# Attention of a decoder step on one core: from single heads to pairs of heads, with the score products cut to 64 rows

## The chip, the cores and the metric

The kernel is one program on one core of a Trainium2 chip. The metric is the time of one execution on the device in microseconds (us), as a median of several runs. The engines work side by side, each through its own list of instructions in a fixed order, and wait for each other through semaphores: TensorE (PE in the profile; PEld is its loading of weights), VectorE (DVE), ScalarE (ACT), GpSimd (POOL) and SyncE (SP), which here issues most DMAs.

## The reference

One layer of a decoder for a prompt of 1024 tokens and 8 samples of 8 new tokens. After the input projection each of 8 heads of 64 channels attends over the prompt. Three dilated window branches are merged by their softmax denominators, which is the same as one softmax over all earlier keys with an added table (bias plus the logarithm of the number of branches that see the key):

```python
    q = rms_norm(q, q_g) * (HEAD_DIM ** -0.5)
    k = rms_norm(k, k_g)
...
        attn = _merge_branches([_dilated_prompt(q, k, v, w, d, rel_bias) for w, d in DILATED_BRANCHES])
...
    mix = jnp.concatenate([attn, pool], axis=-1).astype(x.dtype) @ w_out
    x = x + gate1 * mix
```

The samples attend over a cache of 2048 past rows each, and the rest is a pooling path, an output projection, and a block of two large products (1024 to 4096 channels and back).

## The kernel before, in words

Everything is stored with channels on the 128 partitions. `qT[hp]` and `kT[hp]` hold two heads each, head 2*hp on partitions 0 to 63 and the odd one on 64 to 127. Large products are made in a one-pass form of float32 (F32R) from a high and a low part of each operand; products of plain float32 take two passes over the array, transposes one.

The stage that matters here begins behind the input projection and ends with the first product of the output projection (`oa`, L243). It runs over 32 units, each one head `h` and one group `g` of 256 queries (blocks 2g and 2g+1 of 128):

- `head_prep` makes the parts of q and k for the next head. `qs` holds the high part of q on the head's 64 partitions and its low part on the other 64, `kh` the high part of k on both (the second copy comes by a DMA, L487), `kl` the low part of k and zeros. So qs with kh and qs with kl are two products over 128 rows.
- `unit_S` makes the scores of 128 queries against all keys up to them: L620 and L621 into a PSUM bank (tag `S`, six banks, shared with transposes and the samples' work). `logits` (L536, VectorE) adds the bias tile `fs` of the head and keeps the row maximum, `softmax_tail` (L530, ScalarE) takes the exponential and its row sum, L625 puts the reciprocal on a diagonal `dg`.
- `unit_V` transposes the exponentials (L636), copies them out of PSUM (L639, ScalarE) and multiplies with the values (L641): 64 output channels, so that the two query blocks of the unit stand in two halves of the array's columns (output partitions 0 to 63 and 64 to 127). L644 spreads the reciprocal sums in the same way, L646 copies them, L650 multiplies and writes the result over `qT`.
- One step of the samples' attention goes between: `sample_S` (products of 32 output rows, four column groups, L557) and `sample_V` (L582 transposes, L590 products in four column groups).

The loop issues S of a unit, then V of the unit before it. This is not yet the order on the engines: a scheduler reorders the instructions when the program is built, by its own estimate of when each is ready. `load_bias` (L506) loads 512 KB of the table into `fs`, two buffers, one head ahead. `wp`, the weights of the pooling path's last product (L670, twelve products that fill the end of the stage), is loaded at the start of the stage. `split_mix` makes the high and low parts that the output projection reads.

In what follows a tiling is named as the profile names it, rows x columns of the array that a product takes: 128*128 (S and transposes), 128*64 (V), 128*32 (samples).

## Time and profile before

| what | value |
|---|---|
| median of 3 runs | 1380.88 us (1378.78 to 1387.12) |
| profiled execution | 1385.69 us |
| its span, first to last instruction | 1383.9 us |
| instructions in the span | 22069 |
| TensorE busy | 1323.1 us, 96% |
| mean granted clock of TensorE | 0.981 of 2.4 GHz |

The span and the profiled execution's own time differ by what lies around the instructions. Busy time of TensorE is a union of modelled spans, and its tail after the last column counts as busy; so a busy TensorE can still be one that changes from one tiling to another. Some records of products are missing from a trace, and a row that stands for "x4" may be three of them.

### The profile page before, as it was taken

Reading aid. Unit: us, or ns where it says so; the run is one execution under the profiler, and the core shown is the slowest. Engines: PE = TensorE matmul, PEld = TensorE weight load, DVE = VectorE, ACT = ScalarE, POOL = GpSimd, SP = SyncE. Lnnn points to the kernel's source line nnn. Section 1 sums busy time; section 2 is a strip of 40 time slices with the busy share of each in tenths; the row PEclk is TensorE's granted clock in tenths of the full one; section 3 lists DMA queues with packets and bytes.
Section 4 is the critical chain, followed back from the end, with each engine's and each line's share of the span. In section 5 each row is a group of like instructions: output and inputs, shape, how many; then the busy total and the mean of one; then the engine's idle time right before and its main releaser. Section 6 shows DMA issues by size and latency. Waiting matters only on the chain.

```text
span 1383.9 us, 22069 instructions
## 1 busy us (share of the span) xinstructions
PE 1323.1 (96%) x9284; PEld 1133.3 (82%) x9284; DVE 609.9 (44%) x1266; ACT 404.1 (29%) x708; POOL 142.2 (10%) x200
## 2 busy tenths in 40 slices
PE   3799999798999999999999999999999999999998
PEld 1486868586777768999999999999999999999998
DVE  5644142116767775577332433433433324334333
ACT  5232121125677763435202202112012012021120
POOL 3102004322223200000000000000000000000000
PEclk9799999899999999999999999999999999999999
DMA  9684331949867825481961541721814515411002
GB/s 302 214 148 141 122 122 62 146 129 345 268 234 240 286 80 193 135 283 61 348 203 46 186 148 46 258 76 45 275 46 135 199 46 186 148 46 46 31 33 97
DMA packets 59074, 213.10 MB, mean 154 GB/s; under 512 B 15056, under 2 KB 17104, under 8 KB 57952
## 3 DMA queue, kind: packets, MB, share of 16 engines
q1 hardware_dynamic: 55088, 138.82, 32.3%
q0 software_dynamic: 3888, 72.87, 16.4%
q8 instruction: 73, 1.20, 0.4%
q14 instruction: 25, 0.20, 0.0%
HBM read 199.15 MB, written 77.27 MB: 200 GB/s over the span
## 4 chain that ended last, share of the span: by engine, by line
PE 89%; DMA 4%; ACT 2%; DVE 2%; issue 2%; SPq 1%; POOL 0%; ACTq 0%; DVEq 0%
PE dn L243 9%; PE dn L245 9%; PE dn L247 9%; PE up L247 9%; PE up L243 9%; PE up L245 9%; PE z L243 5%; PE z L247 4%; PE z L245 4%; PE po L641 2%; DMA wa<-in_w_ada 2%; PE pt L636 2%; PE sl L557 1%; PE pa L101 1%; PE ob L245 1%
## 5 line engine op out<-in xcount | busy, mean ns | idle before, releaser
L723 DVE SCALAR_TENSOR_TENSOR X<-dn,aT,X 128x512 f32<-128x512 f32 (+2 forms) x192 | 98.4, 567 | 204.6 <-PE dn L247 204.6
L755 POOL COPY mark<-fh 128x1 f32<-128x1 f32 x7 | 8.5, 1219 | 562.2 <-ACT fh L822 562.2
L823 DVE TENSOR_TENSOR fl<-r,fh 128x1088 fp32r<-128x1088 f32 x32 | 41.3, 1292 | 35.5 <-ACT fh L822 35.5
L530 ACT ACTIVATE L<-L,m 128x128 f32<-128x128 f32 (+3 forms) x64 | 49.8, 778 | 22.2 <-DVE m L536 22.0
L641 PE MATMUL po<-PT,vtok 128*64 128x128 f32 x576 | 52.2, 287 | 4.1 <-ACT PT L639 3.4
L641 PEld LDWEIGHTS po<-PT,vtok 128*64 128x64 f32 x576 | 33.7, 136 | 23.4 <-ACT PT L639 12.9
L822 ACT CAST fh<-r 128x1088 fp32r<-128x1088 f32 x32 | 35.4, 1106 | 44.0 <-DVE r L819 44.0
L101 PE MATMUL pa<-wa,cs 128*32 128x256 f32 x384 | 31.5, 414 | 15.0 <-DMA wa<-in_w_ada 14.9
L639 ACT COPY PT<-pt 128x512 f32<-128x512 f32 (+1 forms) x80 | 40.2, 541 | 16.6 <-PE pt L636 16.4
L245 PE MATMUL dn<-fh,wd_3l 128*128 128x288 f32 (+1 forms) x192 | 43.4, 328 | 0.0
L243 PE MATMUL dn<-fh,wd_3h 128*128 128x288 f32 (+1 forms) x192 | 43.4, 328 | 0.0
L247 PE MATMUL dn<-fl,wd_3h 128*128 128x288 f32 (+1 forms) x192 | 43.4, 328 | 0.0
L243 PE MATMUL dn<-fh,wd_1h 128*128 128x288 f32 (+1 forms) x192 | 42.5, 328 | 0.0
L245 PE MATMUL dn<-fh,wd_1l 128*128 128x288 f32 (+1 forms) x192 | 42.5, 328 | 0.0
L247 PE MATMUL dn<-fl,wd_1h 128*128 128x288 f32 (+1 forms) x192 | 42.3, 328 | 0.0
L245 PE MATMUL dn<-fh,wd_0l 128*128 128x288 f32 (+1 forms) x192 | 42.3, 328 | 0.0
L636 PE MATMUL pt<-cpk,L 128*128 128x128 f32 x288 | 41.6, 281 | 0.7 <-ACT L L530 0.4
L243 PE MATMUL dn<-fh,wd_0h 128*128 128x288 f32 (+1 forms) x192 | 42.2, 328 | 0.0
L243 PE MATMUL dn<-fh,wd_2h 128*128 128x288 f32 (+1 forms) x192 | 42.2, 328 | 0.0
L245 PE MATMUL dn<-fh,wd_2l 128*128 128x288 f32 (+1 forms) x192 | 42.2, 328 | 0.0
L247 PE MATMUL dn<-fl,wd_2h 128*128 128x288 f32 (+1 forms) x192 | 42.2, 328 | 0.0
L247 PE MATMUL dn<-fl,wd_0h 128*128 128x288 f32 (+1 forms) x192 | 42.1, 328 | 0.0
(953 smaller groups left out, 3505.9 us busy)
## 6 DMA issues: line engine op xcount, KB each, us to landing
out_kw<-in_cache_k POOLq DMA_DIRECT2D x8, 4080.0 KB, 16.1
out_vw<-in_cache_v POOLq DMA_DIRECT2D x8, 4080.0 KB, 29.0
wa<-in_w_ada SPq DMA_DIRECT2D x48, 512.0 KB, 5.7
kc<-in_kc SPq DMA_DIRECT2D x40, 512.0 KB, 5.8
vc<-in_vc SPq DMA_DIRECT2D x40, 512.0 KB, 5.7
x<-in_xT SPq DMA_DIRECT2D x8, 544.0 KB, 8.3
X<-in_xT SPq DMA_DIRECT2D x8, 544.0 KB, 7.9
fs<-gscr SPq DMA_DIRECT2D x8, 512.0 KB, 6.4
```

Source lines behind the costliest of these rows:

```text
L101: ins = mm(pa[32 * g:32 * g + 32, :256], cs[:, k, :], t[:, g // 2, (g % 2) * 256:(g % 2 + 1) * 256], start=(k == 0), stop=(k == KD - 1))
L243: mm(pt[:, :n], wh[:, kw], xh(k, c0, n), start=st, stop=False)
L245: mm(pt[:, :n], wl[:, kw], xh(k, c0, n), start=False, stop=False)
L247: mm(pt[:, :n], wh[:, kw], xl(k, c0, n), start=False, stop=sp)
L530: last["act"] = S.activation(L[:, :n], L[:, :n], AF.Exp, bias=negm, scale=-1.0, accum_out=sm)
L557: mm(pt[32 * hp:32 * hp + 32, c0:c0 + 256], qz[:, hp, b, :], kch[:, hp, :], start=True, stop=True)
L636: nc.tensor.transpose(pt[:, n * P:(n + 1) * P], Ls[ii][:, j * P:(j + 1) * P], ident)
L639: S.copy(PT[:, :w], pt[:, :w])
L641: mm(po[E * ii:E * ii + E, :P], v_blk(j, h * E, E), PT[:, n * P:(n + 1) * P], start=(j == 0), stop=(j == 2 * g + ii))
L723: V.scalar_tensor_tensor(X[:, m, c0:c0 + npr], pt[:, :npr], aT[:, base + m, 0:1], X[:, m, c0:c0 + npr], ALU.mult, ALU.add)
L822: S.copy(fh, r)
L823: V.tensor_sub(fl, r, f(fh))
```

## The change

The unit becomes a pair of heads `hp` and a group of 256 queries (16 units in place of 32).

- S: three products over 64 rows (high q with high k, high q with low k, low q with high k) in place of two over 128. Head 0 of the pair takes the upper half of the array's rows, head 1 the lower half, each into a bank of its own. The copy of `kh` by DMA and the zeros in `kl` go; the parts are made for both heads at once on 128 partitions.
- V: the halves of the columns now stand for the two heads, and a product takes both query blocks of the unit, 256 wide (128 for the last key block). `dg` is made in one instruction for two heads and two blocks, and reciprocal, copy and multiplication come once in a unit.
- The exponentials of a unit lie in one tile, with one buffer for even and one for odd `g`; `dg` and `bc` have one buffer. Both `fs` buffers belong to the pair in work, and the loads for the next pair are written in the pair's second unit.
- The samples' steps are dealt out anew (three or four in a unit), `wp` is loaded behind the attention, and the memory for descriptors of software DMAs is halved.

```diff
-    kls = [wpool.tile([P, SEQ], F32R, tag="wf", name=f"kl{a}", bufs=NWF) for a in range(2)]
-    for a in range(2):
-        V.memset(f(kls[a][E - a * E:2 * E - a * E, :]), 0.0)
-
-    def head_prep(h, pieces):
-
-        hp, r0 = h // 2, (h % 2) * E
-        a, b = slice(r0, r0 + E), slice(E - r0, 2 * E - r0)
-        q, k, kl = qT[hp], kT[hp], kls[h % 2]
-        qs, kh = (wpool.tile([P, SEQ], F32R, tag="wf", name=f"{n}{h}", bufs=NWF) for n in ("qs", "kh"))
-        stacks[h] = (qs, kh, kl)
+
+    def pair_prep(hp, pieces):
+
+        q, k = qT[hp], kT[hp]
+        kh, qh, ql = [wpool.tile([P, SEQ], F32R, tag="wf", name=f"{n}{hp}", bufs=NWF) for n in ("kh", "qh", "ql")]
+        kl = nat(f"kl{hp}", F32R)
+        stacks[hp] = kh, kl, qh, ql
         w = SEQ // pieces
         for c0 in range(0, SEQ, w):
             c = slice(c0, c0 + w)
-            S.copy(kh[a, c], k[a, c])
-            nc.sync.dma_start(f(kh[b, c]), f(kh[a, c]))
-            S.copy(qs[a, c], q[a, c])
-            G.tensor_sub(kl[a, c], k[a, c], f(kh[a, c]))
-            G.tensor_sub(qs[b, c], q[a, c], f(qs[a, c]))
+            S.copy(kh[:, c], k[:, c])
+            S.copy(qh[:, c], q[:, c])
+            G.tensor_sub(kl[:, c], k[:, c], f(kh[:, c]))
+            G.tensor_sub(ql[:, c], q[:, c], f(qh[:, c]))
             yield
 
-    for _ in head_prep(0, 2):
+    for _ in pair_prep(0, 2):
...
-        fs = att.tile([P, FW], F32, tag="fs", name=f"fs{h}", bufs=2)
+        fs = att.tile([P, FW], F32, tag="fs", name=f"fs{h}", bufs=NFS)
...
+    load_bias(1)
...
-    def unit_S(h, g):
-        qs, kh, kl = stacks[h]
-        fs = biases[h]
-        out = []
-        dg = att.tile([P, 2 * P], F32, tag="dg", name=f"dg{h}_{g}", bufs=2)
+    def unit_S(hp, g):
+
+        kh, kl, qh, ql = stacks[hp]
+        Ls = {}
+        LL = att.tile([P, 2, (4 * g + 3) * P], F32, tag=f"L{g % 2}", name=f"L{hp}_{g}", bufs=1)
+        sm = att.tile([P, 4], F32, tag="sm4", name=f"sm{hp}_{g}", bufs=4)
         for ii in range(2):
             qi = 2 * g + ii
             nk = (qi + 1) * P
-            L = att.tile([P, SEQ], F32, tag="L", name=f"L{h}_{qi}", bufs=NL)
-            m = None
             n = nk if nk <= 512 else nk // 2
+            nm = max(n, 256)
+            qc = slice(qi * P, (qi + 1) * P)
+            ms = [None, None]
+            for a in range(2):
+                Ls[a, ii] = LL[:, a, ii * (nk - P):ii * (nk - P) + nk]
             for c0 in range(0, nk, n):
-                pt = ps(f"S{h}_{qi}_{c0}", "S")
-                nm = max(n, 256)
-                mm(pt[:, :nm], qs[:, qi * P:(qi + 1) * P], kh[:, c0:c0 + nm], start=True, stop=False)
-                mm(pt[:, :nm], qs[:, qi * P:(qi + 1) * P], kl[:, c0:c0 + nm], start=False, stop=True)
+                pts = [ps(f"S{hp}_{a}_{qi}_{c0}", "S") for a in range(2)]
+                for x, (w, m) in enumerate(((qh, kh), (qh, kl), (ql, kh))):
+                    for a in range(2):
+                        r = slice(a * E, (a + 1) * E)
+                        mm(pts[a][:, :nm], w[r, qc], m[r, c0:c0 + nm], start=(x == 0), stop=(x == 2))
                 b0 = (7 - qi) * P + c0
-                m = logits(L, c0, n, pt[:, :n], fs[:, b0:b0 + n], m, f"m{h}_{qi}_{c0}")
-            rv = softmax_tail(L, nk, m, f"p{h}_{qi}")
-            V.tensor_scalar_mul(dg[:, ii * P:(ii + 1) * P], ident, rv)
-            out.append(L)
-        return out, dg
-
-    def unit_V(h, g, Ls, dg):
-        hp, r0 = h // 2, (h % 2) * E
-        po = ps(f"po{h}_{g}", "po")
+                for a in range(2):
+                    ms[a] = logits(Ls[a, ii], c0, n, pts[a][:, :n], biases[2 * hp + a][:, b0:b0 + n], ms[a],
+                                   f"m{hp}_{a}_{qi}_{c0}")
+            for a in range(2):
+                softmax_tail(Ls[a, ii], nk, ms[a], sm[:, 2 * a + ii:2 * a + ii + 1])
+        rv = att.tile([P, 4], F32, tag="sm4", name=f"rv{hp}_{g}", bufs=4)
+        V.reciprocal(rv, sm)
+        dg = att.tile([P, 4, P], F32, tag="dg", name=f"dg{hp}_{g}", bufs=1)
+        V.tensor_tensor(dg, ident.unsqueeze(1).to_broadcast([P, 4, P]), rv.unsqueeze(2).to_broadcast([P, 4, P]), ALU.mult)
+        return Ls, dg
+
+    def unit_V(hp, g, Ls, dg):
+        po = ps(f"po{hp}_{g}", "po")
         for jp in range(g + 1):
-            pt = ps(f"pt{h}_{g}_{jp}", "S")
-            blocks = [(2 * jp + jj, ii) for jj in range(2) for ii in range(2) if 2 * jp + jj <= 2 * g + ii]
-            for n, (j, ii) in enumerate(blocks):
-                nc.tensor.transpose(pt[:, n * P:(n + 1) * P], Ls[ii][:, j * P:(j + 1) * P], ident)
-            PT = att.tile([P, 512], F32, tag="PT", name=f"PT{h}_{g}_{jp}", bufs=NPT)
-            w = len(blocks) * P
-            S.copy(PT[:, :w], pt[:, :w])
-            for n, (j, ii) in enumerate(blocks):
-                mm(po[E * ii:E * ii + E, :P], v_blk(j, h * E, E), PT[:, n * P:(n + 1) * P],
-                   start=(j == 0), stop=(j == 2 * g + ii))
-        for ii in range(2):
-            mm(po[E * ii:E * ii + E, P:2 * P], ones[:, :E], dg[:, ii * P:(ii + 1) * P], start=True, stop=True)
-        bc = att.tile([P, P], F32, tag="bc", name=f"bc{h}_{g}", bufs=2)
-        S.copy(bc, po[:, P:2 * P])
+            PTs = []
+            js = [(2 * jp + jj, [ii for ii in range(2) if 2 * jp + jj <= 2 * g + ii]) for jj in range(2)]
+            for a in range(2):
+                pt = ps(f"pt{hp}_{a}_{g}_{jp}", "S")
+                n = 0
+                for j, iis in js:
+                    for ii in iis:
+                        nc.tensor.transpose(pt[:, n * P:(n + 1) * P], Ls[a, ii][:, j * P:(j + 1) * P], ident)
+                        n += 1
+                PT = att.tile([P, 512], F32, tag="PT", name=f"PT{hp}_{a}_{g}_{jp}", bufs=NPT)
+                S.copy(PT[:, :n * P], pt[:, :n * P])
+                PTs.append(PT)
+            n = 0
+            for j, iis in js:
+                w = len(iis) * P
+                for a in range(2):
+                    mm(po[E * a:E * a + E, iis[0] * P:2 * P], v_blk(j, (2 * hp + a) * E, E), PTs[a][:, n:n + w],
+                       start=(j == 0), stop=(j == 2 * g + 1))
+                n += w
+        for a in range(2):
+            mm(po[E * a:E * a + E, 2 * P:4 * P], ones[:, :E], dg[:, 2 * a:2 * a + 2, :].rearrange("p s c -> p (s c)"),
+               start=True, stop=True)
+        bc = att.tile([P, 2 * P], F32, tag="bc", name=f"bc{hp}_{g}", bufs=1)
+        S.copy(bc, po[:, 2 * P:])
         mix = qT[hp]
-        for ii in range(2):
-            c = slice((2 * g + ii) * P, (2 * g + ii + 1) * P)
-            V.tensor_tensor(mix[r0:r0 + E, c], po[E * ii:E * ii + E, :P], bc[E * ii:E * ii + E], ALU.mult)
-        if h % 2 and g % 2:
-            if g == 1:
-                mixh[hp], mixl[hp] = nat(f"mixh{hp}", F32R), nat(f"mixl{hp}", F32R)
-            c = slice((g - 1) * 2 * P, (g + 1) * 2 * P)
-            split_mix(hp, c, mix[:, c], G)
+        c = slice(g * 2 * P, (g + 1) * 2 * P)
+        V.tensor_tensor(mix[:, c], po[:, :2 * P], bc, ALU.mult)
+        if g == 3:
+            mixh[hp], mixl[hp] = nat(f"mixh{hp}", F32R), nat(f"mixl{hp}", F32R)
+            for c in (slice(0, 512), slice(512, 1024)):
+                split_mix(hp, c, mix[:, c], G)
 
...
-    wp = att.tile([P, 4, P], F32, tag="wp", name="wp")
-    nc.sync.dma_start(wp, i["wpT"])
...
-    units = [(h, g) for h in range(H) for g in range(4)]
+    units = [(hp, g) for hp in range(HP) for g in range(4)]
     ready = []
-    for n, (h, g) in enumerate(units):
+    s_, v_ = [sample_S(b) for b in range(NB)], [sample_V(b) for b in range(NB)]
+    steps = [s_[0]] * 3 + [s_[1]] * 3 + [v_[0]] * 3
+    for b in range(1, NB):
+        for _ in range(3):
+            steps += ([s_[b + 1]] if b + 1 < NB else []) + [v_[b]]
+    steps = iter(steps)
+
+    def sample_steps(n):
+        for it in itertools.islice(steps, n):
+            next(it, None)
+
+    for hp, g in units:
         if g == 0:
-            if h + 1 < H:
-                load_bias(h + 1)
-            prep = head_prep(h + 1, 4) if h + 1 < H else iter(())
-            sS = itertools.chain(*(sample_S(b) for b in ((0, 1) if h == 0 else (h + 1,)) if b < NB))
-            sV = sample_V(h)
-        ready.append((h, g, *unit_S(h, g)))
-        for _ in range(2 if h == 0 else 1):
-            next(sS, None)
+            prep = pair_prep(hp + 1, 4) if hp + 1 < HP else iter(())
+        if g == 1 and hp + 1 < HP:
+            load_bias(2 * hp + 2)
+            load_bias(2 * hp + 3)
+        ready.append((hp, g, *unit_S(hp, g)))
+        sample_steps((1, 2, 2, 2)[g])
         if len(ready) > 1:
             unit_V(*ready.pop(0))
-        if h or g:
-            next(sV, None)
+        sample_steps((1, 1, 1, 2)[g])
         with tc.issue_after(last["act"].ins):
             next(prep, None)
-    next(sV, None)
     unit_V(*ready.pop(0))
+    sample_steps(48)
     for hp in range(HP):
         sv = attnS[:, hp].rearrange("p b t -> p (b t)")
         split_mix(hp, slice(SEQ, T), sv, V)
+    wp = wpool.tile([P, 4, P], F32, tag="raw", name="wp", bufs=NRAW)
+    nc.sync.dma_start(wp, i["wpT"])
...
-NL = 4
+NFS = 2
...
+    nc = _bacc.Bacc("TRN2", target_bir_lowering=False, num_devices=1, dynamic_dma_scratch_size=8192)
```

TensorE, the scores of query blocks 6 and 7 of the first head (before) or pair (after), between V products of the group before (names: `S_6_0` is block 6, keys from 0, and behind the change `S_0_6_0` that of head 0 in the pair; `po` is V's result, `PT` the copied transposes, `PT_0_1_0` of head 0, group 1, first four blocks; `x4` stands for four products). Before:

```order
L620 MATMUL S_6_0_2652<-kh_2313,qs_2312 128x448
L621 MATMUL S_6_0_2652<-kl_2308,qs_2312 128x448
L641 MATMUL po_1_2591<-PT_1_0_2597,vtok_2041 64x128 x4
L620 MATMUL S_6_448_2657<-kh_2313,qs_2312 128x448
L621 MATMUL S_6_448_2657<-kl_2308,qs_2312 128x448
L620 MATMUL S_7_0_2668<-kh_2313,qs_2312 128x512
L621 MATMUL S_7_0_2668<-kl_2308,qs_2312 128x512
L641 MATMUL po_1_2591<-PT_1_1_2607,vtok_2041 64x128 x3
L644 MATMUL po_1_2591<-dg_1_2415,cpk 64x128 x2
L620 MATMUL S_7_512_2673<-kh_2313,qs_2312 128x512
L621 MATMUL S_7_512_2673<-kl_2308,qs_2312 128x512
```

After:

```order
L621 MATMUL S_0_6_0_2715<-kh_2308,qh_2309 128x448
L621 MATMUL S_0_6_0_2715<-kl_2311,qh_2309 128x448
L621 MATMUL S_0_6_0_2715<-kh_2308,ql_2310 128x448
L653 MATMUL po_1_2642<-PT_0_1_0_2648,vtok_2041 64x256
L621 MATMUL S_1_6_0_2716<-kh_2308,qh_2309 128x448
L621 MATMUL S_1_6_0_2716<-kl_2311,qh_2309 128x448
L621 MATMUL S_1_6_0_2716<-kh_2308,ql_2310 128x448
L653 MATMUL po_1_2642<-PT_1_1_0_2655,vtok_2041 64x256
L653 MATMUL po_1_2642<-PT_0_1_0_2648,vtok_2041 64x256
L653 MATMUL po_1_2642<-PT_1_1_0_2655,vtok_2041 64x256
L621 MATMUL S_0_6_448_2727<-kh_2308,qh_2309 128x448
```

Before, a row of V products holds both halves of the columns. After, three products of one head stand in a row, then those of the other, and V's first product for head 0 stands alone between them.

SyncE, where the bias tiles of the third and fourth head are loaded (`fs2`, `fs3`; the digit behind `kc` and `vc` is the sample). Before, where head 1 is in work:

```order
L579 DMA vc1_0_2843<-in_vc 128x1024
L579 DMA vc1_1_2845<-in_vc 128x1024
L579 DMA vc1_2_2931<-in_vc 128x1024
L506 DMA fs2_2752<-gscr_101 128x1x1024
L487 DMA kh1_2409<-kh1_2409 64x256
L554 DMA kc2_4_2997<-in_kc 128x1024
L554 DMA kc3_0_3181<-in_kc 128x1024
```

After, where the pair of heads 0 and 1 ends:

```order
L574 DMA vc0_4_2771<-in_vc 128x1024
L574 DMA vc1_0_2872<-in_vc 128x1024
L501 DMA fs2_2421<-gscr_101 128x1x1024
L574 DMA vc1_1_2874<-in_vc 128x1024
L501 DMA fs3_2423<-gscr_101 128x1x1024
L574 DMA vc1_2_2952<-in_vc 128x1024
L547 DMA kc2_4_3062<-in_kc 128x1024
L547 DMA kc3_0_3155<-in_kc 128x1024
```

The two loads now stand where the last scores of the pair before have been read, and loads of the samples' values and keys are queued behind them; the copies of `kh` are gone. From the first product of the output projection on, the order on TensorE is the same in both programs.

## Rows read from the trace of the kernel before

**Rows 1.** Page, part 1: busy time, share of the span, instructions.
```profile
PE 1323.1 (96%) x9284; PEld 1133.3 (82%) x9284; DVE 609.9 (44%) x1266; ACT 404.1 (29%) x708; POOL 142.2 (10%) x200
```

**Rows 2.** Windows: length, busy time of each engine, TensorE clock, DMA share, GB/s.
```profile
311.60:522.30 210.70, 199.96 (x2396) 146.53 (x2394) 148.27 (x531) 140.38 (x337) 52.53 (x74) 0.98 0.70 239
522.30:1383.90 861.60, 857.64 (x5192) 780.75 (x5190) 348.21 (x569) 183.46 (x251) 16.76 (x25) 1.00 0.40 133
...
311.00:330.00 19.00, 15.40 (x175) 10.01 (x174) 10.56 (x44) 8.34 (x21) 4.12 (x10) 0.82 1.00 368
```

**Rows 3.** Timeline: start us, length us, S products of 512 and 256 columns.
```profile
409.24 0.40 PE L621 MATMUL S<-kl,qs 128*128 128x512 f32 x1
409.47 0.39 PE L620 MATMUL S<-kh,qs 128*128 128x512 f32 x1
...
340.75 0.28 PE L621 MATMUL S<-kl,qs 128*128 128x256 f32 x1
340.87 0.28 PE L620 MATMUL S<-kh,qs 128*128 128x256 f32 x1
```

**Rows 4.** Timeline of TensorE, V products, normalisation, sample S, transposes.
```profile
412.11 0.39 PE L620 MATMUL S<-kh,qs 128*128 128x256 f32 x1
412.33 0.28 PE L621 MATMUL S<-kl,qs 128*128 128x256 f32 x1
...
413.31 1.07 PE L557 MATMUL sl<-kc,qz 128*32 128x256 f32 x16
414.31 0.33 PE L636 MATMUL pt<-cpk,L 128*128 128x128 f32 x1
414.57 0.44 PE L641 MATMUL po<-PT,vtok 128*64 128x128 f32 x4
414.84 0.27 PE L644 MATMUL po<-dg,cpk 128*64 128x128 f32 x1
414.84 0.27 PE L641 MATMUL po<-PT,vtok 128*64 128x128 f32 x1
...
414.95 0.27 PE L641 MATMUL po<-PT,vtok 128*64 128x128 f32 x1
415.06 0.38 PE L644 MATMUL po<-dg,cpk 128*64 128x128 f32 x2
415.37 1.75 PE L636 MATMUL pt<-cpk,L 128*128 128x128 f32 x14
```

**Rows 5.** Timeline: products of L361, one in each of four row groups.
```profile
196.71 1.13 PE L361 MATMUL qrb<-qrst,cpk 32*128 32x512 f32 x6
197.78 0.42 PE L101 MATMUL pa<-wa,cs 128*32 128x256 f32 x4
```

**Rows 6.** Waits of TensorE in the stage: us in total, times, longest.
```profile
PE po L641 <- ACT PT L639: 3.4, 10, 0.6
PE sl L557 <- DMA kc<-in_kc: 3.3, 2, 2.0
PE spo L590 <- DMA vc<-in_vc: 0.8, 1, 0.8
```

**Rows 7.** Groups by shape, other engines: busy us, mean ns of one.
```profile
L650 DVE TENSOR_TENSOR q<-po,bc 64x128 f32<-64x128 f32 x64 | 18.5, 288 | 7.8 <-ACT bc L646 6.6
L646 ACT COPY bc<-po 128x128 f32<-128x128 f32 x32 | 8.4, 264 | 21.2 <-PE po L644 21.0
L490 POOL TENSOR_TENSOR qs<-q,qs 64x256 fp32r<-64x256 f32 x28 | 20.5, 733 | 2.1
```

**Rows 8.** Loads of the bias tile fs, from issue to landing.
```profile
DMA to landing us min/median/max: 4.7/6.4/8.0
```

**Rows 9.** Groups: end of the stage, pool products, low half of mix.
```profile
L670 PE MATMUL pp<-u,wp 128*128 128x288 f32 (+1 forms) x24 | 8.7, 486 | 0.0
L659 POOL TENSOR_TENSOR mixl<-q,mixh 128x512 fp32r<-128x512 f32 x8 | 10.4, 1300 | 35.2 <-ACT mixh L658 19.1 <-issue 15.8
```

10 lines of the change are left out of this document (4 added, 6 removed).

## The prediction

> **What bounds the kernel now.** I read the page's first part, then windows, then the timeline of TensorE inside the stage that changes. TensorE is busy 96% of the span [rows 1]. Behind the attention it is busy 857.6 of 861.6 us [rows 2], and its order there is the same in both programs, so nothing can be won or lost there. What can move is the stage from the first S product to the first product of the output projection: 210.7 us, in which TensorE is busy 200.0, VectorE 148 and ScalarE 140 [rows 2]. So TensorE bounds the stage, its list of products is the price list, and its 10.7 us of idle time come on top.
>
> **Prices of TensorE.** S, one pass: 512 columns start 0.23 us apart, 256 columns 0.12 [rows 3], which is 0.45 ns a column. Float32, per pass: the two last passes of L644 lie 0.11 apart (0.38 less the 0.27 of a single one) for 128 columns, so 0.85 ns a column [rows 4]; L557 agrees: 16 passes of 256 columns in four column groups, 1.00 us to the next product [rows 4]. A transpose is one such pass. Column groups run beside each other: rows of L641 and L644 start together at 414.84 [rows 4]. They even run out of the written order: L644's first pass (written behind both passes of L641's last product) starts at 414.84, the last of L641 at 414.95 [rows 4]. So each part of the array works off its own list.
>
> Changing the tiling costs time. The last pass of L644 starts at 415.17 (415.06 + 0.11) and takes 0.11, the next transpose starts at 415.37 [rows 4]: 0.09 lost. Then the first weights are not loaded ahead: behind a change two S products of 256 columns lie 0.22 apart (412.11, 412.33 [rows 4]) instead of 0.12, so 0.10 more for 128 columns of weights. For 64 columns it is 0.06 (L641 x4 spreads its starts over 0.44 - 0.27 = 0.17 instead of 0.11 [rows 4]), for 32 I take half of that. So to enter a stretch of 128 weight columns costs 0.20 us, of 64 0.145, of 32 0.12.
>
> **The stage before, as a check of the prices.** For each stretch of one tiling in the built order I take the longest part's list. S: 4,736 columns a head, two products, 8 heads, 75,776 columns: 34.2 us. Transposes and pool products: 49.3 (384 x 0.109, and 7.4). V and normalisation: 41.9 (38.4 if the two halves were always even). Samples: 39.7. Sum 165.1. Stretches entered: 73 of 128 rows and columns, 75 of V, 43 of samples: 30.6. With the idle 10.7 this is 206.4 of 210.7, and the half-clock part of the first 19 us (0.82 granted, that is a share at 1.2 GHz [rows 2]) is most of the rest. The list closes, so I use it for the change.
>
> **The change part by part.** *S.* Three products for two heads at a time: 3 x 4,736 x 4 pairs = 56,832 columns, 25.6 us, if both row groups always run together. No row shows 64-row groups of the one-pass form. The nearest is L361: six recorded passes of 512 columns in four row groups take 1.13 us and the next tiling starts 1.07 behind [rows 5], where six in a row would take 2.6; so row groups do run together, and I take that. The upper bound is all products in a row, 51.3. But the scheduler has not kept the pairs together. Of 45 stretches of S 15 hold one head only, and others are uneven; the longer list in each sums to 74,304 columns: 33.5 us. Against 34.2 S gains 0.7, not 8.6.
>
> *V and normalisation.* The column passes are the same in number, 38.4 us when even. Now a half of the columns is a head, and a head's product comes when its transposes have been copied. In the built order 25 of 64 stretches hold one 256-column product alone (25 x 0.44 = 10.9), the other 39 sum to 40.1: 51.0, against 41.9. This is a loss of 9.1 us; the order of TensorE printed with the change shows one such product. *Samples*: 40.1 against 39.7.
>
> *Tilings.* S was 128*128 like the transposes and is now a tiling of its own. Stretches entered: 45 of S, 48 of transposes and pool, 64 of V, 52 of samples: 34.1 us, against 30.6, 3.5 more. That a change into or out of two row groups costs the same as others rests on L361: 1.07 from its first start to the next tiling is two passes of 0.43 plus 0.21 [rows 5].
>
> So TensorE's list grows by 0.4 + 9.1 - 0.7 + 3.5 = 12.3 us.
>
> *Other engines.* 48 multiplications of 0.29, 16 copies of 0.26, half of the casts and 32 of POOL's 0.73 subtractions go [rows 7], and 32 copies of kh leave SyncE's queue. VectorE and ScalarE had 62 and 70 us of slack in the stage [rows 2]; I count nothing. If TensorE's list grew less than I think, they would still not be next.
>
> *Start.* The first kc loads keep TensorE waiting 3.3 us [rows 6] while the DMAs are full at 368 GB/s [rows 2]. 512 KB (wp and the copies of kh for the first two heads) no longer stand before or between them: 1.4 us less waiting.
>
> *Bias tiles.* fs is no longer loaded a head ahead: at three places both loads start only when the last scores of a pair are read. A load lands 4.7 to 8.0 us after its issue, median 6.4 [rows 8]. In the built order TensorE has 26 rows of other work between the last S of a pair and the first of the next (transposes and V of the group before, samples): 9.2 us by the same list and 2.0 of tilings. Also S of the next pair can run into its banks before VectorE needs fs. So 11.2 us against about 7.5: cost nothing. What is queued behind them on SyncE (vc and kc) is needed later still. If the cover were gone, it would be 7 us at each of three places.
>
> *End.* The last unit is a pair, and its low part of mix is needed by the fourth of eight products of the output projection. Six pool products still stand behind the last normalisation, half of 8.7 us [rows 9], and nine passes of 0.23; the chain behind the normalisation is a copy, a multiplication, a cast, each under a us, and 1.3 on POOL [rows 9]. Nothing.
>
> **Sum.** 12.3 - 1.4 = 10.9 us longer, other waits unchanged. The profiled execution took 1385.69, so 1396.6 for one like it; the median of the runs is 4.8 below it: 1392 us. That is 0.8%, inside the 1% that a measurement of this kernel can tell from no change.
>
> **The rivals.**
>
> (a) *The row groups keep the written order.* Then three products of one head hold up the other's, and groups overlap only where head changes to head. Counted so, S takes 37.8 us: 4.3 more, 1396 us, slower by 1.1%. For it: no row has a one-pass product in row groups. Against it: L644 overtaking L641 [rows 4]. The Trainium skill states this rival as a rule: "TensorE: Matmul & The Clock Gate", section "Part 3: Packing small matmuls — row/col tiling", says that products start and end strictly in program order, whatever tile they go to. By that rule, 1396; the overtaking L644 speaks against it for column groups.
>
> (b) *The row groups do not run together at all*, so the change doesn't do what it says. S is 51.3 us, 17.8 more: 1410 us, slower. L361 speaks against it [rows 5], though in two-pass float32.
>
> (c) *Bias tiles late.* If other loads on the queues delay them past the 11 us, VectorE stands at the first scores of the pair, the banks stay full and TensorE runs dry: at most 3 x 7 = 21 us, half of it 10: 1402, slower by 1.5%. It decides from a landing of some 10 us after issue.
>
> (d) *The uneven stretches fill waits.* A head's product alone is placed where the other head's copy isn't ready; before, TensorE waited there (3.4 us on PT, 10.7 idle in all [rows 2, 6]). If all idle time but the 1.4 already counted goes, 9.3 less: 1382 us, no change.
>
> (e) *Faster.* If there were no drain between S and V, so that heads overlap across stretches, S would be 25.6 and V 38.4: 20.5 less; with (d), 30 less: 1362, faster by 1.4%. Each change of tiling in the rows speaks against it [rows 4, 5].
>
> **How the numbers follow.** My sum 0.50, (a) 0.13, (b) 0.10, (c) 0.08, (d) 0.13, (e) 0.06. The predicted time is the sum's, 1392. Around it I allow 6 us for waits that move, so a third of it lies over the bound of 1% (1394.7). The range goes from 1378, a little under (d), to 1407, which takes in (a), most of (c) and leaves out (b) and (e): 0.16 to 0.2 outside. Slower by over 1%: 0.13 + 0.10 + 0.08 and 0.15 of the sum's, 0.46. Within 1%: 0.35 + 0.13 = 0.48. Faster: 0.06.
>
> **What would show it.** In the changed profile: rows of S of the two heads that start within 0.01 us of each other, also where three of one head are written first (else (a) or (b)); a window of the stage near 221 us with TensorE idle about 9; V's products with starts of 0.22 and, alone, without a partner; 0.2 us at each change of tiling; no TensorE wait on fs or on VectorE at the three pair changes (else (c)). The prediction is wrong if idle time before hides what I count as work, or if tilings cost less between row and column groups than in the rows.

## The result and the profile after

The changed kernel takes 1406.09 us (median of 4 runs, 1401.62 to 1409.29), the kernel before on the same chip 1380.7 (1378.78 to 1387.12): ratio 1.0172, 95% interval 1.0146 to 1.0198. It is slower by 1.7%, where 0.8% was forecast.

First the windows of the changed kernel, cut where the first S product of each head pair, the first pool product and the first product of the output projection start; then the sixth row is the whole stage, the seventh all that follows it. Columns: window, its length, busy time of PE, PEld, DVE, ACT and POOL (instructions), granted TensorE clock, DMA share, GB/s.

```profile
305.50:354.80 49.30, 42.42 (x397) 25.49 (x396) 24.96 (x88) 25.38 (x60) 10.11 (x15) 0.93 0.77 264
354.80:409.20 54.40, 51.55 (x540) 33.52 (x538) 26.77 (x90) 30.34 (x70) 8.69 (x12) 0.97 0.68 220
409.20:463.50 54.30, 51.50 (x538) 33.66 (x536) 26.65 (x90) 30.39 (x70) 8.53 (x12) 0.97 0.65 214
463.50:528.50 65.00, 59.48 (x655) 42.10 (x653) 33.45 (x102) 35.17 (x76) 2.71 (x3) 0.95 0.52 175
528.50:541.40 12.90, 12.90 (x51) 6.12 (x50) 8.79 (x16) 5.27 (x11) 1.27 (x1) 1.00 0.20 75
305.50:541.40 235.90, 217.85 (x2169) 140.89 (x2168) 120.63 (x386) 126.56 (x287) 31.31 (x43) 0.96 0.62 207
541.40:1403.10 861.70, 857.56 (x5191) 780.75 (x5190) 348.79 (x570) 183.45 (x251) 16.21 (x24) 1.00 0.39 133
```

The same cuts in the kernel before, whose sum is in [rows 2]:

```profile
311.60:361.90 50.30, 45.49 (x567) 32.74 (x566) 32.44 (x127) 29.57 (x71) 11.78 (x21) 0.93 0.96 340
361.90:411.10 49.20, 47.11 (x595) 35.44 (x594) 33.66 (x125) 33.50 (x83) 13.99 (x20) 1.00 0.71 242
411.10:459.40 48.30, 47.49 (x594) 35.28 (x592) 34.33 (x127) 33.67 (x84) 14.53 (x21) 1.00 0.74 252
459.40:510.60 51.20, 48.17 (x574) 35.95 (x575) 38.32 (x132) 36.97 (x87) 11.34 (x14) 1.00 0.51 167
510.60:522.30 11.70, 11.70 (x71) 7.12 (x70) 9.52 (x22) 6.67 (x17) 0.89 (x1) 1.00 0.11 43
```

The stage is 235.9 us long instead of 210.7, so 25.2 longer; the rest behind it is 861.7 against 861.6 [rows 2]. The first S product starts 6.1 us earlier than in the profile of before, but this is no gain of the change: in the profiles of the twelve kernels below, whose code ahead of the stage is the same, it starts anywhere from 302.6 to 311.4. The difference of the stages, 25.2, is the difference of the medians, 25.4; the stage is therefore what the experiments are compared by.

**Three parts of 25.2.** *Idle*: length less busy time of TensorE, 18.1 us against 10.7: 7.4 more. *Clock*: in windows of about 1 us through the stage I sum length times (1 less the granted clock), which is what work at 1.2 GHz costs: 10.2 us against 3.4, 6.8 more. (A wait inside a half-clock stretch is in both sums, 0.5 us in either kernel; run 4 below has most, 3.3.) *Work*, busy time less that: 207.6 against 196.5, 11.1 more. By pairs the clock column shows where: 0.97, 0.97 and 0.95 in the second to fourth pair, 1.00 in all of before.

Names in what follows: `sl` are the samples' scores, `spt` the transposes of their exponentials, `sPT` the copies of these out of PSUM, `spo` the products of sPT with the values, `os` the normalised result and `sot` its transpose. The waits of TensorE in the stage (us in total, times, longest), to be read against [rows 6] and one more row of the kernel before:

```profile
PE sot L596 <- DVE os L594: 1.5, 2, 0.8
```

After:

```profile
PE spo L585 <- DVE sPT L580: 7.7, 5, 2.9
PE sot L591 <- DVE os L589: 5.1, 8, 1.1
PE S L621 <- POOL kl L484: 1.9, 1, 1.9
PE sl L550 <- DMA kc<-in_kc: 1.5, 1, 1.5
PE S L621 <- DVE ms L529: 1.2, 2, 1.0
PE po L653 <- ACT PT L647: 0.5, 1, 0.5
```

The wait for PT copies has fallen from 3.4 to 0.5 us and that for kc from 3.3 to 1.5; waits for VectorE have come in or grown: for the samples' sPT (7.7) and os (1.5 to 5.1). Where the largest one stands, the timeline shows (start, length; rows of other lines and the 0.08 us reads of the accumulator left out):

```profile
390.15 0.63 DVE L529 CUSTOM_DVE_ANT_0 L<-S,fs 128x448 f32<-128x448 f32 x1 [0.47 <-PE S L621]
...
392.46 0.68 DVE L529 CUSTOM_DVE_ANT_0 L<-S,fs 128x512 f32<-128x512 f32 x1
...
393.07 0.68 DVE L631 TENSOR_TENSOR dg<-cpk,rv 128x512 f32<-128x512 f32 x1
...
393.68 0.68 DVE L529 CUSTOM_DVE_ANT_0 L<-S,fs 128x512 f32<-128x512 f32 x1
...
394.17 0.55 PE L577 MATMUL spt<-cpk,Ls 128*128 128x128 f32 x3
...
394.29 0.74 DVE L529 CUSTOM_DVE_ANT_0 L<-S,fs,m 128x512 f32<-128x512 f32 x1
...
394.96 0.42 DVE L663 TENSOR_TENSOR q<-po,bc 128x256 f32<-128x256 f32 x1
...
395.29 0.74 DVE L529 CUSTOM_DVE_ANT_0 L<-S,fs,m 128x512 f32<-128x512 f32 x1
...
395.96 0.55 DVE L580 COPY sPT<-spt 128x384 f32<-128x384 f32 x1
...
396.56 0.65 PE L585 MATMUL spo<-vc,sPT 128*32 128x128 f32 x16 [1.85 <-DVE sPT L580]
...
400.03 3.37 PE L644 MATMUL pt<-cpk,L 128*128 128x128 f32 x22
```

At the end of a pair (unit g = 3) VectorE has eight logits in a row, both heads', besides dg and a mult: four of 448 columns from 390.15 to 392.46, then those shown, without a gap. TensorE is done with the S products, does the sample's three transposes spt, and the next thing written for it is spo, which needs their copy: it stands behind the row. Behind the wait 22 transposes take 3.37 us; in a kernel below, at full clock, the same 22 take 2.57. The same wait ends at 450.92 (1.9 us) and at 507.09 (2.9); in the last one a subtraction for the output projection's weights (1.22 us, at 504.68) stands in VectorE's row too.

### The profile page after: what moved, and what is told of

Same layout as the page of the kernel before. It is cut to its first block, busy times and chain, and to the rows that moved or that the text cites. A ratio compares the mean times of both kernels' runs of the same rounds, so it can differ in the third digit from the quotient of the medians.

```text
span 1403.1 us, 21249 instructions
## 1 busy us (share of the span) xinstructions
PE 1337.8 (95%) x9060; PEld 1125.3 (80%) x9060; DVE 581.1 (41%) x1120; ACT 390.7 (28%) x660; POOL 116.4 (8%) x168
## 4 chain that ended last, share of the span: by engine, by line
PE 90%; DMA 4%; DVE 4%; issue 1%; ACT 1%; SPq 1%; POOL 0%; DVEq 0%; POOLq 0%; ACTq 0%
PE dn L245 9%; PE dn L247 9%; PE dn L243 9%; PE up L243 9%; PE up L245 9%; PE up L247 9%; PE z L243 4%; PE z L247 4%; PE z L245 4%; PE po L653 3%; PE pt L644 2%; PE S L621 2%; PE sl L550 1%; DMA wa<-in_w_ada 1%; PE spo L585 1%; PE ob L245 1%
## 5 line engine op out<-in xcount | busy, mean ns | idle before, releaser
L525 ACT ACTIVATE L<-L,m 128x128 f32<-128x128 f32 (+7 forms) x64 | 49.2, 769 | 50.7 <-DVE m L529 50.4
L653 PE MATMUL po<-PT,vtok 128*64 128x256 f32 (+1 forms) x320 | 58.1, 378 | 0.5 <-ACT PT L647 0.5
L653 PEld LDWEIGHTS po<-PT,vtok 128*64 128x64 f32 x320 | 25.3, 137 | 22.0 <-issue 10.7
L243 PE MATMUL dn<-fh,wd_0h 128*128 128x288 f32 (+1 forms) x192 | 42.2, 328 | 0.0
L243 PE MATMUL dn<-fh,wd_2h 128*128 128x288 f32 (+1 forms) x192 | 42.2, 328 | 0.0
L245 PE MATMUL dn<-fh,wd_2l 128*128 128x288 f32 (+1 forms) x192 | 42.2, 328 | 0.0
L247 PE MATMUL dn<-fl,wd_2h 128*128 128x288 f32 (+1 forms) x192 | 42.2, 328 | 0.0
L247 PE MATMUL dn<-fl,wd_0h 128*128 128x288 f32 (+1 forms) x192 | 42.2, 328 | 0.0
L101 PE MATMUL pa<-wa,cs 128*32 128x256 f32 x384 | 31.0, 410 | 10.7 <-DMA wa<-in_w_ada 10.7
L839 DVE TENSOR_TENSOR r<-r 128x1088 f32<-128x1088 f32 x32 | 41.1, 1285 | 0.0
```

The lines of the kernel that those rows point to most:

```text
L101: ins = mm(pa[32 * g:32 * g + 32, :256], cs[:, k, :], t[:, g // 2, (g % 2) * 256:(g % 2 + 1) * 256], start=(k == 0), stop=(k == KD - 1))
L243: mm(pt[:, :n], wh[:, kw], xh(k, c0, n), start=st, stop=False)
L245: mm(pt[:, :n], wl[:, kw], xh(k, c0, n), start=False, stop=False)
L247: mm(pt[:, :n], wh[:, kw], xl(k, c0, n), start=False, stop=sp)
L525: last["act"] = S.activation(L[:, :n], L[:, :n], AF.Exp, bias=negm, scale=-1.0, accum_out=sm)
L653: mm(po[E * a:E * a + E, iis[0] * P:2 * P], v_blk(j, (2 * hp + a) * E, E), PTs[a][:, n:n + w], start=(j == 0), stop=(j == 2 * g + 1))
```

## The experiments

All in one table. "Counted" is the list of TensorE in the built order by the prediction's prices; work, idle and clock loss are taken from each profile as above, and with the stage's length they add up. Ratios are to the kernel before on the same chip (1382.8 us beside runs 1 to 4, 1381.1 beside 5 to 8, 1379.8 beside 9 to 12), in brackets the 95% interval; so times of different groups compare only to some 3 us.

| kernel | us | ratio | stage | counted | work | idle | clock |
|---|---|---|---|---|---|---|---|
| before | 1380.7 | | 210.7 | 195.7 | 196.5 | 10.7 | 3.4 |
| after | 1406.1 | 1.0172 [1.0146, 1.0198] | 235.9 | 208.1 | 207.6 | 18.1 | 10.2 |
| 1 steps late | 1407.2 | 1.0179 [1.0156, 1.0201] | 236.5 | 203.4 | 206.4 | 21.6 | 8.5 |
| 2 V paired | 1391.9 | 1.0059 [1.0037, 1.0081] | 219.3 | 183.9 | 183.7 | 23.6 | 11.9 |
| 3 sample end apart | 1400.0 | 1.0122 [1.0096, 1.0147] | 227.6 | 207.5 | 207.3 | 15.2 | 5.1 |
| 4 S alone, heads together | 1426.6 | 1.0313 [1.0283, 1.0343] | 252.5 | 193.7 | 193.8 | 42.2 | 16.4 |
| 5 sPT on ScalarE | 1408.7 | 1.0191 [1.0155, 1.0227] | 239.2 | 211.4 | 210.3 | 17.0 | 12.0 |
| 6 S alone, head by head | 1406.0 | 1.0175 [1.0125, 1.0224] | 243.9 | 184.9 | 186.3 | 35.3 | 22.2 |
| 7 = 2 + 3 | 1376.7 | 0.9965 [0.9946, 0.9985] | 206.4 | 182.4 | 183.2 | 18.0 | 5.1 |
| 8 = 7 + 5 + mix earlier | 1380.3 | 0.9987 [0.9970, 1.0005] | 207.6 | 182.5 | 184.6 | 17.9 | 5.1 |
| 9 wait filled | 1404.6 | 1.0173 [1.0155, 1.0190] | 234.7 | 213.3 | 213.3 | 16.3 | 5.1 |
| 10 weights held | 1407.1 | 1.0202 [1.0177, 1.0227] | 239.5 | 208.1 | 207.5 | 18.3 | 13.6 |
| 11 = 7 + 10 | 1370.8 | 0.9934 [0.9918, 0.9949] | 201.9 | 182.4 | 183.5 | 15.0 | 3.4 |
| 12 = 6 + 1 + 3 | 1394.3 | 1.0100 [1.0081, 1.0118] | 225.0 | 186.8 | 192.1 | 27.8 | 5.1 |

**1. The sample's steps later.**

```diff
-        sample_steps((1, 2, 2, 2)[g])
+        sample_steps((1, 2, 2, 0)[g])
...
-        sample_steps((1, 1, 1, 2)[g])
+        sample_steps((1, 1, 1, 4)[g])
```

> Edit: in the last unit of a head pair (g = 3) no sample step is dealt ahead of the V part and four after it, instead of two and two; nothing else. Theory 1 (the VectorE queue): in the changed kernel the eight logits of that unit, two heads of four, its dg and the unit before's mult stand ahead of the sPT copy on VectorE, and TensorE, with nothing else written ahead, waits for sPT 1.9, 1.9 and 3.0 us at 394, 449 and 504 us, and runs behind each such wait for some us at a granted clock of 0.5 (windows of 0.77 and 0.80, 0.60, 0.50 and 0.72). With 22 transposes of the unit before written there instead, the three waits and the half-clock stretches behind them go: 6.8 us and about as much again, so 1393 us (1390 to 1398). Its list of TensorE work is 4 us shorter too, by the count of products and tilings, so the low end is likelier. Rival: the wait is for the bias tiles of the next pair, which are loaded at that point (two rows at 395.06); then the steps change nothing and the time stays at 1404 to 1408. Second rival: VectorE is late whatever stands behind, and the transposes only move the wait to the V products: 1402 to 1406.

No faster. In the second and third pair the half-clock stretches are gone and a pair takes 52.5 and 52.1 us instead of 54.4, but TensorE now waits in each for a PT copy on ScalarE (0.8 us), besides 1.9 us in all for sPT and os in each. The last pair is 4.5 us longer (82.4 from its first S product to the output projection, 77.9 before the edit): the four steps that were put off stand in a heap there, and TensorE waits 4.4 us for vc loads. The bias rival has nothing for it, since the pair changes did get shorter; the second rival, that the wait moves, is nearest.

**2. V products in fixed pairs.**

```diff
                 w = len(iis) * P
-                for a in range(2):
-                    mm(po[E * a:E * a + E, iis[0] * P:2 * P], v_blk(j, (2 * hp + a) * E, E), PTs[a][:, n:n + w],
-                       start=(j == 0), stop=(j == 2 * g + 1))
+                def v_mm(a):
+                    return mm(po[E * a:E * a + E, iis[0] * P:2 * P], v_blk(j, (2 * hp + a) * E, E), PTs[a][:, n:n + w],
+                              start=(j == 0), stop=(j == 2 * g + 1))
+                with tc.issue_after(v_mm(1).ins):
+                    v_mm(0)
```

> Edit: of the two heads' V products of one block of keys the product of head 1, whose transposed logits come last, is written first and that of head 0 queued right behind it on TensorE; nothing else. Theory 1 (the list): the changed kernel loses 9 us on its V and normalisation stretches because 25 of the 64 hold one head alone, 10.9 us of single products. Counted with the prices of the prediction, the list falls from 208.1 to 183.9 us: V and normalisation 51.0 to 38.4, changes of tiling 34.1 to 28.0, S 33.5 to 30.7 since fewer V stretches cut through it. If TensorE does not wait for the later copies instead: 1382 us; if it waits 0.2 us at each of 40 stretches: 1390. Rival: the lone products stood where TensorE would have waited anyway, for the copy of the second head or for VectorE, and the time stays at 1402 to 1408. The waits for sPT stay in either case.

Work falls by 23.9 us, where 24.2 was counted: the lone V products and the stretches that they cut were what the prediction took them for. Of this 5.5 us come back as idle and 1.7 at half clock: 16.6 us off the stage. The time lies 2 us over the end with 0.2 us of waiting.

**3. The end of a sample apart.**

```diff
+        tails.append(lambda: sample_end(b, po))
+        yield
+
+    def sample_end(b, po):
         os_ = att.tile([P, P], F32, tag="os", name=f"os{b}", bufs=2)
...
         for it in itertools.islice(steps, n):
+            old = tails[:]
+            tails.clear()
             next(it, None)
+            for t in old:
+                t()
```

> Edit: the end of a sample (os on VectorE, its transpose sot and the two copies into attnS) is written after the sample step that follows, not right behind the last spo; nothing else. Theory: the eight waits of TensorE for os, 0.55 to 1.14 us, 5.7 us in all, are one more part of the loss (two of 0.8 us stood there before the change); with other products between they go, less 0.1 to 0.2 us for each added change of tiling: 1401 us (1399 to 1403). Rival: VectorE is the one that is late, and what TensorE does not wait for os it waits for the next copy: 1404 to 1408.

It gains 6.1 us, within the forecast range. The waits for os hardly fell (5.1 to 4.6 us); those for sPT did, 7.7 to 4.4, and the clock loss halved. In the new order sixteen sl products stand between spt and spo:

```profile
399.12 0.55 PE L577 MATMUL spt<-cpk,Ls 128*128 128x128 f32 x3
399.60 1.07 PE L550 MATMUL sl<-kc,qz 128*32 128x256 f32 x16
401.51 0.64 PE L585 MATMUL spo<-vc,sPT 128*32 128x128 f32 x16 [0.85 <-DVE sPT L580]
...
403.02 2.57 PE L649 MATMUL pt<-cpk,L 128*128 128x128 f32 x22
```

So the step did help, though by another wait than the one that the theory named.

**4. S alone, the two heads' V parts side by side.**

```diff
-        po = ps(f"po{hp}_{g}", "po")
+        pos = [ps(f"po{hp}_{a}_{g}", "po") for a in range(2)]
...
-                    mm(po[E * a:E * a + E, iis[0] * P:2 * P], v_blk(j, (2 * hp + a) * E, E), PTs[a][:, n:n + w],
-                       start=(j == 0), stop=(j == 2 * g + 1))
...
+                        mm(pos[a][E * ii:E * ii + E, :P], v_blk(j, (2 * hp + a) * E, E), PTs[a][:, n:n + P],
+                           start=(j == 0), stop=(j == 2 * g + ii))
```

> Edit: the V part and the normalisation as before the change (products of 128 queries, the two blocks of queries of one head in the two column groups, one normalisation, one bc and two mults for each head), S and the units as after it. Theory 1: the V part as changed costs 9.1 us by its lone products; undone, the list is 193.7 us against 208.1 (V 51.0 to 41.9, S 33.5 to 30.4, changes of tiling 34.1 to 30.7), the waits at the end of each pair and the half-clock stretches behind them stay, so 1392 us (1388 to 1396). Rival: the whole loss is the waits and the clock; then the old V part changes nothing, or costs 1 to 3 us more for VectorE's smaller mults and ScalarE's twice as many bc copies: 1404 to 1410.

A clear miss: 20 us slower than the changed kernel. The work is as counted (193.8 of 193.7), but TensorE idles for 42.2 us. In this form a unit holds both po banks, and the samples' products need one too; that this is the cause is argued, not shown (the waits name sPT, 13.8 us, exponentials, 5.9, os, 5.7, and vc loads, 5.5). Run 6 does it head by head.

**5. The sPT copies on ScalarE.**

```diff
-            V.tensor_copy(PT[:, :w], pt[:, :w])
+            S.copy(PT[:, :w], pt[:, :w])
```

> Edit: the 22 copies sPT of the samples' transposes on ScalarE instead of VectorE; nothing else. Theory 1 (VectorE's queue at the end of a pair): four waits of TensorE for sPT, 7.8 us, and the half-clock stretches behind three of them come from eight logits, dg and a mult that stand ahead of the copy on VectorE, without a gap from 392.46 to 396.51 in the changed kernel; ScalarE had 0.7 us free there (394.39 to 395.07). Then the waits fall to 3 us or less and the time at half clock from 20.4 to about 12 us; the list is 3.3 us longer by the count of tilings: 1400 us (1396 to 1404). Rival: ScalarE, with two activations of 1.15 us and bc in its queue, is as late; the waits stay and the longer list shows: 1407 to 1411.

The rival holds. The wait at the pair change is 2.0 us, where it was 1.9, and now for ScalarE, where the copy stands behind an exponential that itself waited for VectorE's logits:

```profile
399.33 1.15 ACT L525 ACTIVATE L<-L,m 128x1024 f32<-128x1024 f32 x1 [0.68 <-DVE m L529]
...
400.48 0.46 ACT L580 COPY sPT<-spt 128x384 f32<-128x384 f32 x1
...
400.99 0.64 PE L585 MATMUL spo<-vc,sPT 128*32 128x128 f32 x16 [2.02 <-ACT sPT L580]
```

So it is not one engine's queue. Both engines still hold the softmax of a unit twice as large as before, and TensorE has been written nothing to do meanwhile.

**6. S alone, head by head.** (The normalisation, cut here, goes back to one head at a time too.)

```diff
-        po = ps(f"po{hp}_{g}", "po")
-        for jp in range(g + 1):
+        for a in range(2):
+            r0 = a * E
+            po = ps(f"po{hp}_{a}_{g}", "po")
+            for jp in range(g + 1):
...
+                for n, (j, ii) in enumerate(blocks):
+                    mm(po[E * ii:E * ii + E, :P], v_blk(j, (2 * hp + a) * E, E), PT[:, n * P:(n + 1) * P],
+                       start=(j == 0), stop=(j == 2 * g + ii))
```

> Edit: S and the units as after the change, the V part as before it and one head after the other, as before (each head its transposes, products of 128 queries, its normalisation, bc and mults); unlike the run in which the two heads' V parts ran side by side, a unit never holds both of the banks named po at one time, which the samples' products need too. Theory: there the list was right (191 us of work) and 45 us of waits, many at po, ate it; here the list is 184.9 us, the shortest so far. If the waits are as in the changed kernel (19.5 us, and 10 us of half clock): stage 213, 1384 us. Rival: the waits grow as the list shrinks, since VectorE's row of eight logits, and four bc and eight mults in each unit, set the end of each pair: 30 us of waits and 12 of half clock: stage 226, 1396 us. Second rival: as the run with the two heads side by side, 1420 or more.

The time of the changed kernel, with 21 us less work: 17.2 us more idle and 12.0 more at half clock took its place. The largest waits:

```profile
PE spo L585 <- DVE sPT L580: 19.1, 7, 5.4
PE spo L585 <- DMA vc<-in_vc: 5.3, 5, 1.9
PE sot L591 <- DVE os L589: 3.7, 8, 0.5
```

The profiled execution was one of the longer runs (span 1412.8), so the stage is some us too long here.

**7 and 8. Edits put together.** Run 7 is the edits of 2 and 3, run 8 besides that of 5 and this:

```diff
-        if g == 3:
-            mixh[hp], mixl[hp] = nat(f"mixh{hp}", F32R), nat(f"mixl{hp}", F32R)
-            for c in (slice(0, 512), slice(512, 1024)):
-                split_mix(hp, c, mix[:, c], G)
+        if g % 2:
+            if g == 1:
+                mixh[hp], mixl[hp] = nat(f"mixh{hp}", F32R), nat(f"mixl{hp}", F32R)
+            c = slice((g - 1) * 2 * P, (g + 1) * 2 * P)
+            split_mix(hp, c, mix[:, c], G)
```

> Edit: the V products of the two heads in fixed pairs and the end of a sample apart, both edits of earlier runs together. List 182.4 us. Theory: the edits act on different things (the list, and the waits at a sample's end), so they add up: stage 235.9 - 16.6 - 8.3 = 211, 1381 to 1384 us, the time of the kernel before. Rival: with the shorter list TensorE meets VectorE earlier, and what the second edit took is waited for elsewhere: 1390 to 1394.

> Edit: as the run with V products in pairs and the end of a sample apart, and besides the sPT copies on ScalarE, and the first half of a pair's mixh and mixl written after its second unit and not with the second half after its fourth. Theory: the waits for sPT go as in the run with that copy alone, and the 2.7 us between the last pool product and the first output projection in the run with paired V products, where TensorE waited for the pair's four GpSimd subtractions, goes too: stage 200 to 206, 1371 to 1378 us. Rival: ScalarE is now the engine that is late (126 us busy and 13 more): 1383 to 1392.

Run 7 is faster than both kernels, by 0.35% in the case of the one before: the two edits add up and more (29.5 us off the stage, 16.6 + 8.3 alone). The largest wait left in it is that for os, 6.1 us, which the second edit was written to take away. Run 8 gains nothing on it. Its waits for sPT are 4.2 us as in run 7 (4.0). The wait ahead of the output projection that was read from run 2, absent in run 7, stands in run 8 with 2.7 us and names VectorE's copies of the pool products, not the GpSimd subtractions: that expectation was wrong.

**9. The wait filled with work that nobody needs.** (`t_` is the last transpose spt; the spo products are queued behind it in the same way.)

```diff
+            if j4 == 8 and b in (2, 4, 6):
+                dm = ps(f"dm{b}", "S")
+                with tc.issue_after(t_.ins):
+                    for n in range(16):
+                        t_ = nc.tensor.transpose(dm[:, n % 4 * P:(n % 4 + 1) * P], ident, ident)
```

> Edit: between the last transposes spt of the samples 2, 4 and 6 and the spo products that wait for their copy, TensorE does 16 transposes of ident into a bank that nobody reads, 1.7 us by the prediction's price of a transpose; they add work that the reference does not ask for, and take away nothing. Theory: the three waits (1.9, 1.9, 3.0 us) cost twice, once as waits and again because TensorE works at a granted clock of 0.5 for some us behind each; with work in the wait the time stays as long but the stretches behind the first two at least, 1.7 us of loss each, and behind the third, 3.4 us, go: stage 229 to 233, 1399 to 1403 us. Rival: the clock falls for another reason than the waits; then nothing changes or the added work shows: 1406 to 1411.

The second to fourth pair get shorter with work added to them: TensorE (timeline), then the windows of the three pairs.

```profile
393.08 0.55 PE L577 MATMUL spt<-cpk,Ls 128*128 128x128 f32 x3
393.47 1.91 PE L582 MATMUL dm<-cpk 128*128 128x128 f32 x16
395.48 0.64 PE L591 MATMUL spo<-vc,sPT 128*32 128x128 f32 x16
```

```profile
353.70:406.50 52.80, 51.70 (x556) 34.34 (x554) 26.78 (x90) 30.24 (x70) 8.71 (x12) 1.00 0.67 226
406.50:459.20 52.70, 51.64 (x554) 34.30 (x552) 26.67 (x90) 30.24 (x70) 8.54 (x12) 1.00 0.68 221
459.20:522.30 63.10, 58.46 (x671) 41.27 (x669) 33.47 (x102) 34.99 (x76) 2.71 (x3) 1.00 0.55 181
```

All three at a clock of 1.00, and shorter by 1.6, 1.6 and 1.9 us. So the slow stretches follow from the waits; run 1 fits, where they went in the second and third pair as no wait there was longer than 1.0 us. In the profile the sum over these three is 5.1 us; 3.9 of them were lost to the start (51.1 against 49.3) and the pool part (15.0 against 12.9), which the edit does not touch. The time, 1404.6, is 1.5 us below that of the changed kernel, but the ratio is the same (1.0173 and 1.0172): in the whole time no gain is shown. The expectation in us was missed, that of the clock met.

**10. The output projection's weights held back.**

```diff
-        wh, wl = load_w(i["w_out"][m], f"wo{name}{m}")
+        with tc.issue_after(last["act"].ins):
+            wh, wl = load_w(i["w_out"][m], f"wo{name}{m}")
```

> Edit: the ScalarE casts of the output projection's weights (woa0h, woa1h, woa2h) are queued behind the last exponential of attention; TensorE's order stays word for word. Theory: in the last pair of the changed kernel the casts (1.04 us each, one of them waiting for its DMA) and the two VectorE subtractions that follow them (1.22 and 2.00 us, at 504.68 and 506.95) stand in the row of logits, exponentials and copies that TensorE waits for; the wait of 3.0 us at 504 falls to the 1.9 us of the other pairs, that of 1.07 to 0.55, and the half-clock time behind it from 6.7 us to about 3.4: 3 us less, 1403 us (1399 to 1404). Rival: the logits set that wait alone; 1405 to 1408.

A miss. The wait of 2.9 us did fall to 1.9, but two waits for vc loads, 2.7 us together, stand in the last pair instead; why stays open. This profile tells something else: its second and third pair have the same waits, 1.9 us for sPT and 1.0 for os in each.

```profile
362.00:416.40 54.40, 51.55 (x540) 33.76 (x538) 26.79 (x90) 30.44 (x70) 8.70 (x12) 0.97 0.65 215
416.40:469.10 52.70, 49.90 (x538) 32.56 (x536) 26.67 (x90) 30.24 (x70) 8.54 (x12) 1.00 0.67 219
```

A wait of 1.9 us took the clock down in the one and not in the other.

**11. Runs 7 and 10 together.**

> Edit: V products in fixed pairs, the end of a sample apart, and the weights' casts held back until behind the last exponential. Theory: in the run with the first two edits the last pair holds 5.5 us of waits and 3.4 us of loss at half clock, the largest a wait of 2.3 us for a PT copy that stands on ScalarE behind the cast of woa1, which itself waits 0.94 us for its DMA; that wait and the stretch behind it go: 1376.7 - 5 = 1371 us (1369 to 1374). Rival: the casts and subtractions only come later, when the last unit's copies and the pool stretch want ScalarE and VectorE, and the time stays at 1376 to 1378.

As expected: 1370.8 us, 0.7% faster than the kernel before. Waits for os (5.8 us) and sPT (4.2) are the largest left. In run 7 TensorE waited like this, with the cast itself waiting for its load:

```profile
477.66 1.04 ACT L146 CAST woa1h<-woa1r 128x1024 fp32r<-128x1024 f32 x1 [0.94 <-DMA woa1r<-in_w_out]
478.61 0.47 ACT L652 COPY PT<-pt 128x384 f32<-128x384 f32 x1
...
479.13 1.55 PE L658 MATMUL po<-PT,vtok 128*64 128x256 f32 x8 [2.34 <-ACT PT L652]
```

In run 11 the copy starts at 471.27, right behind its transposes; the same eight products take 0.87 us at full clock, without a wait:

```profile
472.78 0.87 PE L658 MATMUL po<-PT,vtok 128*64 128x256 f32 x8
```

**12. S alone, with something written ahead of spo.**

> Edit: S and units as changed, the V part as before and head by head, and besides the sample steps of the pair's last unit dealt behind its V part, and the end of a sample apart. Theory: that run without the last two edits had the shortest list of the single edits (it measured 184.6 us of work by its trace) and lost it to 37 us of waits, 20 of them at spo for sPT, and 22 us at half clock, because TensorE has nothing written between the transposes spt and the products behind them while VectorE still has the eight logits in its row. With the V part written there: waits 22, half clock 9, list 186.8: stage 216, 1387 us (1382 to 1392). Rival: VectorE and ScalarE set the time of a pair whatever the order; the waits move to the V products and the time stays at 1400 or above.

The edits of 6, 1 and 3 together; the time lies between the forecast and the rival. Against run 6 the waits for sPT fall from 19.1 to 4.8 us, and the clock loss from 22.2 to 5.1: that part of the theory holds. But waits for vc loads grow from 5.3 to 8.9 us (six), 4.2 come in for PT copies, and the work is 5.3 over its count, so 1394 and not 1387.

## Why the prediction was wrong

The step that failed stands in the sum: "12.3 - 1.4 = 10.9 us longer, other waits unchanged". The 12.3 held (11.1 measured); the waits did not stay, and a cost behind them had no term: 7.4 us more idle and 6.8 us more at half clock, 14.2 in all, on top of work. That 1406.1 still lies in the range stated, 1378 to 1407, is luck: its upper end was set by rivals (a) and (c), and neither came.

- *TensorE's list.* Right, and it stays right through all fourteen kernels: counted and measured work differ by 3 us or less, but for run 12 (5.3). What a built order costs TensorE, waits apart, can be counted from the rows of the kernel before.
- *S.* Row groups run beside each other. Two products of 448 columns are started every 0.20 us, which by the prediction's 0.45 ns a column is the time of one:

```profile
389.76 0.37 PE L621 MATMUL S<-kh,ql 64*128 64x448 f32 x2
...
389.96 0.37 PE L621 MATMUL S<-kh,qh 64*128 64x448 f32 x2
...
390.16 0.37 PE L621 MATMUL S<-kl,qh 64*128 64x448 f32 x2
```

  Rivals (a) and (b) fall with this; the rows of (a)'s place are these, where three products of head 0 are written ahead of head 1's (at half clock from 312.85 on):

```profile
312.43 0.74 PE L621 MATMUL S<-kh,qh 64*128 64x384 f32 x2 [0.15 <-DVE m L529]
312.71 0.39 PE L621 MATMUL S<-kl,qh 64*128 64x384 f32 x1
312.90 0.52 PE L621 MATMUL S<-kh,ql 64*128 64x384 f32 x1
312.97 0.52 PE L621 MATMUL S<-kl,qh 64*128 64x384 f32 x1
```

  The two first products (kh with qh) of both heads start before the second of head 0: head 1's overtook two that are written ahead of it. The page "TensorE: Matmul & The Clock Gate" of the Trainium skill, section "Part 3: Packing small matmuls — row/col tiling", says that products start in program order; these rows differ, and the measurement decides.
- *V.* The loss by lone products was real and was the largest term: run 2 takes it away.
- *Other engines.* "I count nothing" was the wrong reading of slack. VectorE is busy 120.6 us of 235.9 and ScalarE 126.6, less than before, and yet TensorE waits for them, since a unit twice as large gives them its softmax in one row (eight logits where a head's unit had four). The total of an engine says nothing of a queue at one place. That the doubling is the cause is read from VectorE's row, without a gap from 390.15 to 396.51, and fits runs 3, 5 and 12; no smaller unit was tried, so it is argued and not shown. One buffer for dg is another part of the change: VectorE waits 9.7 us for it in 11 places of the stage, but not in its row at any of the three pair changes.
- *Clock.* No term at all. A wait of 1.9 us cost up to 1.7 us again, one of 2.9 us 3.4.
- *Start.* The wait for kc fell by 1.8 us, 1.4 was forecast (the 512 KB of that term are wp and the copies for the first head alone; with the second head's they would be 768); but S now comes before its POOL subtractions are through (1.9) and waits for banks (1.2). First pair: 6.9 us idle against 4.8.
- *Bias tiles*, rival (c): VectorE waits for no fs row in the stage. Right; the waits at the pair changes that (c) would have shown were others.
- *End.* Right: 861.7 against 861.6.
- *The median.* Taking 4.8 us off, because the profiled run lay above the median, did no harm: by stages, 1380.7 + 25.2 = 1405.9, against 1406.1 measured.
- Rival (d) had the sign of the idle time wrong: uneven stretches did not fill it. (e) did not come either; the tilings cost what the rows said.

## What to carry to other kernels

Count the bounding engine's list from the built order, then read its waits again: for each thing that it waits for, ask what is written between the instruction that asks for it and the one that needs it, and how long the queue of the engine in between is at that place, not on average. When units are merged, that queue can grow with the unit while the work to cover it shrinks. And price a wait of TensorE of a few us above its length, for the work behind it may run at half clock: here a pair of heads was 1.6 us shorter in the profile with 1.7 us of useless products than with a wait of 1.9, though the time of the whole kernel does not show it.
